# The second part of split weights, finished by an adding DMA instead of VectorE

## The chip, the cores and the metric

The kernel runs on one core of a Trainium2 chip. The metric is the device time of one execution, in microseconds (us); less is better. Engines are named as in the profile: PE is TensorE (PEld its weight loads), DVE is VectorE, ACT is ScalarE, POOL is GpSimd, SP is the engine that issues nearly all DMAs.

## The reference

A two-layer trunk on 512 tokens of width 1024, in float32. Cut to what matters here:

```python
for i in range(DEPTH):                       # 2 layers
    h = rms_norm(x, attn_norm[i])
    proj = h @ w_in[i]                       # one input projection per layer
    mix = diff_attention(...) if i == 0 else gla_attention(...)
    cross = memory_cross_attention(mem_q, mem, mem_norm[i], w_mem_kv[i], mem_qk_norm[i])
    x = x + concat([mix, cross]) @ w_out[i]
    h = rms_norm(x, ffn_norm[i])
    u = causal_conv3(h @ w_up[i]) + conv_b[i]        # depthwise, width 3
    a, g = split(u, 2)
    x = x + (silu(g) * a) @ w_down[i]
```

All large products multiply activations with float32 weights that are read once from DRAM: `w_in`, `w_mem_kv`, `w_out`, `w_up` (1024 x 5632) and `w_down` (2816 x 1024).

## The kernel before, in words

**Products in three parts.** TensorE multiplies in the type float32r, which keeps fewer bits than float32. So each operand is split into a first part (rounded to float32r, `hi`) and a second part (the rest, `lo`), and each product is the sum of three matmuls: hi by hi, hi by lo, lo by hi. In `product` (L262) the weight's `lo` comes third, in `gemm` (L239) second. The matmuls stand at L267 to L269 and at L250 to L252.

**Weight blocks.** The host packs the weights into `wpack`, one block of 128 partitions by up to 1024 columns (`WTILE`) per load, in the order of use. A piece (`_pieces`) is what one step of the program multiplies with, and has one to four blocks: four of 1024 columns for a projection of the attention part (two K tiles of 128 rows each), two for an up-projection (`ua`, `ug`: four K tiles of 256 columns each), three for a down-projection.

**Refilling.** `weights(key)` hands out a piece and makes sure that the next one is already written into the program (`make_piece`). For each block `make_piece` loads a `raw` tile by SP's queue (L207), ACT casts it to `whi` (L200), and DVE subtracts, `wlo` = `raw` - `whi` (L201). There are 3 buffers for `raw`, and 5 (`WB`) each for `whi` and `wlo`. So a block waits for the matmuls that read the block five before it. The first piece and the one after it are made in the opening part, with tiles of their own (L366 to L409).

**Order of the work.** TensorE's instructions keep the order of the program. The other engines' queues are ordered by a scheduler, except in the opening part. In the attention parts a `Filler` queues the units of the projections and puts them between the steps of attention (`F.fill`). In the feed-forward part (`ffn`, L1001) each step q has a piece `ua` and a piece `ug`, used by turns for two output tiles n; ACT and DVE evaluate the convolution from the results (L1017 to L1021), the gate (L1047, L1048) and the split for the next product (L1050, L1051). After six and five steps follow four down-projection pieces each.

**Other users of the queues.** GpSimd has few instructions: memsets of `bt` (L606), `u` (L1005) and others, and sums of squares (L335) in parts of the second layer. SP issues loads and the stores of results.

Of the kernel before, what the change touches and what calls it, by code (L numbers as in the profile page):

```python
# [10 lines left out]
F32 = mybir.dt.float32  # L11
# [3 lines left out]
ALU = mybir.AluOpType  # L15
# [113 lines left out]
def trunk(ctx, tc, x_t, mem_t, wpack, cols_a_d, cols_d, conv_d, gate_d, rel_bias, diff_lambda, consts, onehot, out):  # L129
    nc = tc.nc  # L130
    mm = nc.tensor.matmul
    V, A, G = nc.vector, nc.scalar, nc.gpsimd
# [23 lines left out]
    def blk(b, w=128):  # L156
        return slice(w * b, w * b + w)
# [39 lines left out]
    at = [0]  # L197

    def split_weights(c, raw, hi, lo):
        A.copy(hi[:, c], raw[:, c])  # L200
        V.tensor_sub(lo[:, c], raw[:, c], hi[:, c].bitcast(F32))  # L201

    def raw_tile():
        return wp.tile([128, WTILE], F32, name="raw", tag="raw", bufs=3)

    def load_raw(raw, n):
        nc.sync.dma_start(raw[:, :n], wpack[at[0], :, :n])  # L207
        at[0] += 1
        return raw

    def make_piece(raws=None):
        parts = []
        for i, (_, _, kk, _, w) in enumerate(blocks[len(made)]):
            n = len(kk)
            raw = load_raw(raw_tile(), n * w) if raws is None else raws[i]
            hi, lo = (wp.tile([128, WTILE], F32R, name=t, tag=t, bufs=WB) for t in ("whi", "wlo"))
            split_weights(slice(0, n * w), raw, hi, lo)
            parts += [(hi[:, blk(j, w)], lo[:, blk(j, w)]) for j in range(n)]
        made.append(parts)

# [2 lines left out]
    def weights(key):  # L223
        i = used[0]
        assert plan[i][0] == key, (plan[i][0], key)
        while len(made) < min(i + 2, len(plan)):
            make_piece()
        used[0] += 1
        parts, made[i] = made[i], None
        return parts  # L230
# [123 lines left out]
    with tc.tile_pool(name="ini", bufs=1) as ip, tc.manual_schedule(engines={E.Activation, E.DVE, E.Pool, E.SP}):  # L354
# [11 lines left out]
        raws = [ip.tile([128, WTILE], F32, name=f"raw{i}") for i in range(4)]  # L366
# [34 lines left out]
        for k in range(KT):  # L401
            if k + 1 < KT:
                operands(k + 1)
            if k == 0:
                second.append(load_raw(raws[0], WTILE))
            if k == 4:
                bias_rows(rb, oh, bs)
            if k == KT - 2:
                make_piece(second)  # L409
                weights(("qk", 0))  # L410
                token_rsqrt("lg", acc[0], NB, r_x[:, 0])
                small_vectors()
                for c in range(2):
                    load(bias_d[:, 512 * c:min(512 * c + 512, 640)], bs[c])
            hi, lo = parts[k]
            terms = (xh[k], hi), (xh[k], lo), (xl[k], hi)
            todo = [(b, i) for b in range(NB) for i in range(3)]
            for b, i in sorted(todo, key=lambda bi: bi[1]) if k == 0 else todo:
                xp, w = terms[i]
                mm(first[b], xp[:, blk(b)], w, start=k == 0 and i == 0, stop=k == KT - 1 and i == 2)  # L420
# [736 lines left out]
```

## Time and profile before

| | |
|---|---|
| time, median of 3 runs | 1204.51 us (1204.1 to 1205.91) |
| the profiled execution: time | 1205.31 us |
| the profiled execution: span | 1203.5 us |
| granted TensorE clock | 1.00 |
| read from HBM, written | 112.63 MB, 4.21 MB |

The span runs from the first to the last instruction of the program; the execution's time is somewhat longer. In the profile a group's line has the place in the code, the engine, the operation, what it writes and reads, the count, and then the busy time in us with the mean length of one in ns, and the idle time of the engine just ahead of these instructions with what ended it. The timeline has the start in us, the length in us, then the same names. A matmul's end is modelled: matmuls are shown as 0.39 us long and start every 0.23 us, so their starts are what counts. The line of a DMA issue has the median time from issue to landing at its end; a `DMA ... landing` line has minimum, median and maximum.

### The profile page before, as it was taken

Reading aid. Unit: us, or ns where it says so; the run is one execution under the profiler, and the core shown is the slowest. Engines: PE = TensorE matmul, PEld = TensorE weight load, DVE = VectorE, ACT = ScalarE, POOL = GpSimd, SP = SyncE. Lnnn points to the kernel's source line nnn. Section 1 sums busy time; section 2 is a strip of 40 time slices with the busy share of each in tenths; the row PEclk is TensorE's granted clock in tenths of the full one; section 3 lists DMA queues with packets and bytes.
Section 4 is the critical chain, followed back from the end, with each engine's and each line's share of the span. In section 5 each row is a group of like instructions: output and inputs, shape, how many; then the busy total and the mean of one; then the engine's idle time right before and its main releaser. Section 6 shows DMA issues by size and latency. Waiting matters only on the chain.

```text
span 1203.5 us, 14757 instructions
## 1 busy us (share of the span) xinstructions
PE 1188.3 (99%) x5672; PEld 975.0 (81%) x5672; DVE 759.8 (63%) x1259; ACT 540.7 (45%) x915; POOL 23.5 (2%) x37
## 2 busy tenths in 40 slices
PE   9999999999999999999999999999999999999998
PEld 6887777778888888888787888987888888888887
DVE  7566578887776534767546446768677653476741
ACT  6666666554444222434436444536444432243420
POOL 0000000000000000000020000003000000000000
PEclk9999999999999999999999999999999999999999
DMA  8432231232332331422342221234233233232231
GB/s 275 132 101 84 80 118 49 71 105 88 98 112 70 123 105 53 130 80 88 116 146 74 70 71 57 62 127 133 78 98 112 71 123 97 67 122 84 87 114 44
DMA packets 39413, 117.80 MB, mean 98 GB/s; under 512 B 4688, under 2 KB 5769, under 8 KB 39343
## 3 DMA queue, kind: packets, MB, share of 16 engines
q1 hardware_dynamic: 39198, 116.60, 30.5%
q8 instruction: 44, 0.72, 0.2%
q10 hardware_dynamic: 144, 0.26, 0.1%
q14 instruction: 27, 0.21, 0.1%
HBM read 112.63 MB, written 4.21 MB: 97 GB/s over the span
## 4 chain that ended last, share of the span: by engine, by line
PE 90%; DVE 5%; ACT 3%; issue 1%; DMA 1%; SPq 0%; DVEq 0%; ACTq 0%
PE ps_mm L268 8%; PE ps_mm L269 8%; PE ps_mm L267 8%; PE ps_sm L267 6%; PE ps_sm L268 6%; PE ps_sm L269 6%; PE ps_mm L250 6%; PE ps_mm L252 6%; PE ps_mm L251 5%; PE ps_tp L267 3%; PE ps_tp L268 3%; PE ps_tp L269 3%; PE ps_lg L268 3%; PE ps_lg L269 3%; PE ps_lg L267 3%; PE ps_tp L169 2%
## 5 line engine op out<-in xcount | busy, mean ns | idle before, releaser
L200 ACT CAST whi<-raw 128x1024 fp32r<-128x1024 f32 (+2 forms) x214 | 207.7, 976 | 247.5 <-PE ps_tp L268 133.8
L201 DVE TENSOR_TENSOR wlo<-raw,whi 128x1024 fp32r<-128x1024 f32 (+2 forms) x214 | 240.8, 1136 | 111.0 <-ACT whi L200 109.9
L267 PE MATMUL ps_mm<-xsh,whi 128*128 128x512 f32 x460 | 182.5, 397 | 0.2 <-DVE xt L969 0.2
L268 PE MATMUL ps_mm<-xsl,whi 128*128 128x512 f32 x460 | 179.4, 390 | 1.4 <-DVE xsl L234 1.3
L269 PE MATMUL ps_mm<-xsh,wlo 128*128 128x512 f32 x460 | 179.3, 390 | 0.0
L268 PE MATMUL ps_sm<-xsl,whi 128*128 128x512 f32 x372 | 144.7, 389 | 0.0
L267 PE MATMUL ps_sm<-xsh,whi 128*128 128x512 f32 x372 | 144.7, 389 | 0.0
L269 PE MATMUL ps_sm<-xsh,wlo 128*128 128x512 f32 x372 | 144.7, 389 | 0.0
L250 PE MATMUL ps_mm<-whi,xsh 128*128 128x512 f32 (+2 forms) x352 | 138.2, 393 | 0.1
L252 PE MATMUL ps_mm<-whi,xsl 128*128 128x512 f32 (+2 forms) x352 | 131.4, 373 | 0.3 <-DVE xsl L234 0.3
L251 PE MATMUL ps_mm<-wlo,xsh 128*128 128x512 f32 (+2 forms) x352 | 130.6, 371 | 0.0
L1019 ACT ACTIVATE cvo<-u,cv 128x512 f32<-128x512 f32 x88 | 71.6, 815 | 114.0 <-DVE u L1017 113.6
L268 PEld LDWEIGHTS ps_mm<-xsl,whi 128*128 128x128 f32 x460 | 86.5, 188 | 20.2 <-DVE xsl L234 2.7
L267 PEld LDWEIGHTS ps_mm<-xsh,whi 128*128 128x128 f32 x460 | 86.4, 188 | 18.2 <-DVE xt L969 0.9
L269 PEld LDWEIGHTS ps_mm<-xsh,wlo 128*128 128x128 f32 x460 | 86.3, 188 | 18.1
L1020 DVE SCALAR_TENSOR_TENSOR cvo<-u,cv,cvo 128x512 f32<-128x512 f32 x88 | 65.9, 749 | 31.6 <-ACT cvo L1019 31.4
L268 PEld LDWEIGHTS ps_sm<-xsl,whi 128*128 128x128 f32 x372 | 69.8, 188 | 14.6
L269 PEld LDWEIGHTS ps_sm<-xsh,wlo 128*128 128x128 f32 x372 | 69.8, 188 | 14.5
L267 PEld LDWEIGHTS ps_sm<-xsh,whi 128*128 128x128 f32 x372 | 69.8, 188 | 14.4
L252 PEld LDWEIGHTS ps_mm<-whi,xsl 128*128 128x128 f32 x352 | 66.1, 188 | 12.7 <-DVE xsl L234 0.5
L250 PEld LDWEIGHTS ps_mm<-whi,xsh 128*128 128x128 f32 x352 | 66.3, 188 | 10.7 <-issue 0.9
L251 PEld LDWEIGHTS ps_mm<-wlo,xsh 128*128 128x128 f32 x352 | 66.5, 189 | 9.5
(247 smaller groups left out, 1767.9 us busy)
## 6 DMA issues: line engine op xcount, KB each, us to landing
raw<-in_wpack_dram SPq DMA_DIRECT2D x176, 512.0 KB, 3.5
raw<-in_wpack_dram SPq DMA_DIRECT2D x27, 256.0 KB, 3.5
xt<-in_x_t_dram SPq DMA_DIRECT2D x16, 256.0 KB, 5.3
xres<-xt SPq DMA_DIRECT2D x8, 256.0 KB, 3.5
xt<-xres SPq DMA_DIRECT2D x8, 256.0 KB, 4.4
out_dram<-xt SPq DMA_DIRECT2D x8, 256.0 KB, 2.0
bt<-bias_d SPq DMA_DIRECT2D x6, 256.0 KB, 5.2
raw<-in_wpack_dram SPq DMA_DIRECT2D x4, 384.0 KB, 2.9
```

Source lines behind the costliest of these rows:

```text
L169: nc.tensor.transpose(dst, src, ident[:n, :n])
L200: A.copy(hi[:, c], raw[:, c])
L201: V.tensor_sub(lo[:, c], raw[:, c], hi[:, c].bitcast(F32))
L250: mm(p, sh[k][:, blk(b)], hi, start=k == 0, stop=False)
L251: mm(p, sh[k][:, blk(b)], lo, start=False, stop=False)
L252: mm(p, sl[k][:, blk(b)], hi, start=False, stop=k == KT - 1)
L267: mm(p, hi[:, blk(n)], bh, start=i == first, stop=False)
L268: mm(p, hi[:, blk(n)], bl, start=False, stop=False)
L269: mm(p, lo[:, blk(n)], bh, start=False, stop=i == last)
L1019: A.activation(c, u[:, 2:], AF.Identity, scale=cv[l][:, 2, j:j + 1], bias=cv[l][:, 3, j:j + 1])
L1020: V.scalar_tensor_tensor(c, u[:, 1:S + 1], cv[l][:, 1, j:j + 1], c, op0=ALU.mult, op1=ALU.add)
```

## The change

In `make_piece`, for all blocks but those of the opening, `wlo` is made in another way. ACT casts `raw` to `whi` as before. Then ACT writes the negative of `whi` into `wlo`, and a DMA on GpSimd's queue reads the same block from `wpack` in DRAM once more and adds it onto `wlo`. `wlo` = -`whi` + block is the value that the subtraction gave. A `raw` tile has then only the cast as its reader. DVE has no part in these blocks any more. The blocks of the opening still go through `split_weights`.

```diff
     def make_piece(raws=None):
         parts = []
         for i, (_, _, kk, _, w) in enumerate(blocks[len(made)]):
             n = len(kk)
+            c = slice(0, n * w)
             raw = load_raw(raw_tile(), n * w) if raws is None else raws[i]
             hi, lo = (wp.tile([128, WTILE], F32R, name=t, tag=t, bufs=WB) for t in ("whi", "wlo"))
-            split_weights(slice(0, n * w), raw, hi, lo)
+            if raws is None:
+                A.copy(hi[:, c], raw[:, c])
+                A.mul(lo[:, c], hi[:, c].bitcast(F32), -1.0)
+                G.dma_start(lo[:, c], wpack[at[0] - 1, :, c], accum_op=ALU.add)
+            else:
+                split_weights(c, raw, hi, lo)
             parts += [(hi[:, blk(j, w)], lo[:, blk(j, w)]) for j in range(n)]
         made.append(parts)
```

## The prediction

> **What bounds the kernel now.** I read the page first, then who waited for whom, then the timeline of single weight blocks.
>
> ```profile
> span 1203.5 us, 14757 instructions
> PE 1188.3 (99%) x5672; PEld 975.0 (81%) x5672; DVE 759.8 (63%) x1259; ACT 540.7 (45%) x915; POOL 23.5 (2%) x37
> ...
> q1 hardware_dynamic: 39198, 116.60, 30.5%
> ...
> PE 90%; DVE 5%; ACT 3%; issue 1%; DMA 1%; SPq 0%; DVEq 0%; ACTq 0%
> ...
> L200 ACT CAST whi<-raw 128x1024 fp32r<-128x1024 f32 (+2 forms) x214 | 207.7, 976 | 247.5 <-PE ps_tp L268 133.8
> L201 DVE TENSOR_TENSOR wlo<-raw,whi 128x1024 fp32r<-128x1024 f32 (+2 forms) x214 | 240.8, 1136 | 111.0 <-ACT whi L200 109.9
> ...
> raw<-in_wpack_dram SPq DMA_DIRECT2D x176, 512.0 KB, 3.5
> ```
>
> TensorE is busy 99% of the span and holds 90% of the chain that ended last. VectorE is busy for 63%. So the 241 us that L201 takes on VectorE are not on the path that sets the end, and taking them away can return only what TensorE now waits. That is little: in the answer for L201 the only one who waited for a wlo is a weight load, for 0.4 us, and the largest waits of the weight loads for VectorE are two short lines.
>
> ```profile
> who waited for it (us, times):
>   PEld ps_lg L613: 0.4, 1
> ...
> PEld ps_mm L268 <- DVE xsl L234: 2.7, 3, 1.6
> PEld ps_lg L800 <- DVE xt L805: 2.1, 2, 1.3
> ```
>
> What matters is how long a refilled block takes. There are five whi and five wlo buffers, so a block can only be refilled when TensorE has let go of the one five blocks earlier, and then has a limited margin until TensorE wants it.
>
> **What changes for a block.** The instruction order of the built kernel shows 203 blocks changed, 172 of them 128x1024; TensorE's order is the same. For each, VectorE's subtraction goes. ScalarE gets a second instruction of the same size, GpSimd's queue an issue, and the DMA engines a second reading of the block from DRAM, added into SBUF. The prices nearest to these:
>
> ```profile
> L207 SPq DMA_DIRECT2D raw<-in_wpack_dram x207: 327/328/587, 13.1 to 1169.2; - x104
> DMA to landing us min/median/max: 2.0/3.5/5.7
> L335 POOL TENSOR_TENSOR xt<-xt 128x512 f32<-128x512 f32 x12 | 19.1, 1588 | 380.0 <-ACT xt L333 375.7 <-issue 3.7 <-POOL xt L335 0.4
> L333 ACT ACTIVATE xt<-xt 128x512 f32<-128x512 f32 x36 | 22.0, 621 | 0.0
> ```
>
> *The negative.* It is a 128x1024 pass on ScalarE like the cast, which the timelines below show at 1.05 us; an activation of half that width takes 0.62 us, so at most some 1.3. I take 1.05, high end 1.5. In all that is about 200 us more for ScalarE (L200 takes 207.7): 740 us, 61%. Its length is hidden under matmuls; its latency is not.
>
> *The issue.* The trace has no DMA on GpSimd's queue. Bounds: 0.33 us, as on SP, and 1.6 us, as a tensor operation there. I take the middle, 1.0. Between the additions stand only memsets of bt and, in the second layer, L335 sums, each among blocks with time to spare.
>
> *The adding transfer.* The trace has none of these either. Payload first: the queue of the loads held 30.5% of 1203.5 us for 116.6 MB, so a 512 KB load (0.524 MB) holds the engines 1.65 us. An addition has two operands, the block in DRAM and what stands in SBUF; as two such streams it is 3.3 us, which I take. Ends: 1.65 (the second stream free) and 4.95 (two reads and the write one after the other). Landing: the load's median 3.5 us plus another 1.65 is 5.2; ends 3.5 and 7.0. The Trainium skill, "Collectives: The Full Stack" (section "The bandwidth ceiling"), says that a reducing transfer runs at half a copy's rate, because of its two source reads and not of the sum; by it 3.3 is right. The skill's "DMA: Bandwidth & Descriptors" (section "Anatomy of one DMA — SWDGE (gpsimd) path") gives about 2.0 us plus the bytes over 436 GB/s for a DMA of GpSimd; taken over both streams that is an estimated 4.4 us in place of my 5.2, and the forecast below would be about 20 us lower. No run so far shows which.
>
> So from the end of the cast to a finished wlo: now 1.23 us, after the change 1.05 + 1.0 + 5.2 = 7.25, that is 6.0 later. And each block holds the DMA engines 1.65 + 3.3 = 4.95 us, where it held them 1.65; blocks refilled close together wait for each other at that pace.
>
> **Stage by stage.** Each fence shows casts, subtractions and the matmuls that first read the part in question.
>
> First layer's attention, one piece of four blocks (the last three refilled together):
>
> ```profile
> 51.54 1.05 ACT L200 CAST whi<-raw 128x1024 fp32r<-128x1024 f32 x1 [0.52 <-PE ps_mm L252]
> 55.13 1.05 ACT L200 CAST whi<-raw 128x1024 fp32r<-128x1024 f32 x1 [0.30 <-PE ps_mm L252]
> 56.22 1.23 DVE L201 TENSOR_TENSOR wlo<-raw,whi 128x1024 fp32r<-128x1024 f32 x1 [0.55 <-ACT whi L200]
> 58.03 0.39 PE L251 MATMUL ps_mm<-wlo,xsh 128*128 128x512 f32 x1
> 62.06 0.39 PE L251 MATMUL ps_mm<-wlo,xsh 128*128 128x512 f32 x1
> ```
>
> The cast waits for TensorE, so it can't start earlier. Third block: wlo done at 57.45, first read at 62.06, a margin of 4.6 us. New: the first block is issued at 51.54 + 2.1 + 1.0 = 54.64 and lands at 59.84, already 1.8 after 58.03; the third lands 9.9 later at 69.7, 7.7 after 62.06. Five pieces in this layer have such margins (4.2 to 5.8 by the same reading): 5 x 7.7 = 39 us.
>
> Second layer's projections, third block of the tightest of six pieces:
>
> ```profile
> 706.21 1.03 ACT L200 CAST whi<-raw 128x1024 fp32r<-128x1024 f32 x1
> 706.45 2.35 DVE L201 TENSOR_TENSOR wlo<-raw,whi 128x1024 fp32r<-128x1024 f32 x2
> 712.42 0.39 PE L251 MATMUL ps_mm<-wlo,xsh 128*128 128x512 f32 x1
> ```
>
> The margin is 3.6 (708.8 to 712.4). I take 7 us for three pieces like it and 1 for the other three, whose blocks lie further apart: 24 us.
>
> First layer's up-projections, one pair of pieces:
>
> ```profile
> 478.13 2.00 ACT L200 CAST whi<-raw 128x1024 fp32r<-128x1024 f32 x2
> 480.02 0.81 ACT L1019 ACTIVATE cvo<-u,cv 128x512 f32<-128x512 f32 x1
> 483.08 2.12 ACT L200 CAST whi<-raw 128x1024 fp32r<-128x1024 f32 x2 [2.24 <-issue]
> 479.46 2.35 DVE L201 TENSOR_TENSOR wlo<-raw,whi 128x1024 fp32r<-128x1024 f32 x2
> 483.51 0.39 PE L269 MATMUL ps_sm<-xsh,wlo 128*128 128x512 f32 x1
> 484.19 0.39 PE L269 MATMUL ps_mm<-xsh,wlo 128*128 128x512 f32 x1
> 489.63 0.39 PE L269 MATMUL ps_mm<-xsh,wlo 128*128 128x512 f32 x1
> ```
>
> In the new order both casts come before the first negative: it ends at 478.13 + 2.0 + 1.05 = 481.2, lands at 487.4, and 484.19 becomes 487.4: 3.2 us. For the second pair of casts a convolution's activation (0.81) and the second cast also stand ahead of the negative: landing 493.25 against 489.63 + 3.2, another 0.4. Of eleven pairs I count ten: 36 us.
>
> Second layer's up-projections, where three blocks are refilled 2.7 us apart with a larger margin, and down-projections (last two lines):
>
> ```profile
> 895.25 1.06 ACT L200 CAST whi<-raw 128x1024 fp32r<-128x1024 f32 x1 [0.89 <-PE ps_sm L268]
> 896.21 0.63 ACT L1047 ACTIVATE cvo<-cvo 128x512 f32<-128x512 f32 x1
> 902.29 1.22 DVE L201 TENSOR_TENSOR wlo<-raw,whi 128x1024 fp32r<-128x1024 f32 x1
> 912.05 0.39 PE L269 MATMUL ps_mm<-xsh,wlo 128*128 128x512 f32 x1
> ...
> 980.86 1.23 DVE L201 TENSOR_TENSOR wlo<-raw,whi 128x1024 fp32r<-128x1024 f32 x1 [2.96 <-ACT whi L200]
> 991.32 0.39 PE L269 MATMUL ps_lg<-midh,wlo 128*128 128x512 f32 x1
> ```
>
> First block: 895.25 + 1.05 + 0.63 + 1.05 + 1.0 + 5.2 = 904.2; the third 9.9 later, 914.1, 2.0 after 912.05. Nine pairs: 18 us. Down: 982.1 + 6.0 = 988.1, before 991.32: nothing. The same holds for the output projections, whose blocks are small and early.
>
> Sum: 39 + 24 + 36 + 18 = 117 us of new TensorE waits, less some 3 us of those for VectorE: +114. The profiled execution took 1205.3 us (1.8 outside its span), 0.8 above the median of 1204.5: **1319 us** for the forecast.
>
> Low end (0.33, 3.5, and 3.3 us per block): third block at 51.54 + 2.1 + 0.33 + 3.5 + 6.6 = 64.1, 2.0 late, five times 10; second layer's three pieces 8; up-projections 485.0 against 484.19, 8; else nothing: 26 less 3, **1228**. High end (1.5, 1.6, 7.0, and 6.6 us per block): 5 x 13.8 = 69, 48, ten times 6.5 = 65, nine times 8.2 = 74, and in the down-projections three blocks hold the engines 19.8 us where TensorE needs 72 matmuls at 0.227 (483.51 to 484.19 are three), 16.4: fourteen times 3.4, 48. Together 304: **1509**.
>
> **Rivals.**
> 1. *The DMA engines become the bound.* For: nothing shows that an addition keeps to twice a load, and from 3.8 us on (5.45 for 24 matmuls less 1.65) the feed-forward stages run at the engines' pace. Against: the engines are now at 30.5%. Time: the high end, about 1510, more if the addition is slower still. Chance 0.28.
> 2. *Faster.* The addition lands as quickly as the fastest load, 2.0 us: 1.05 + 0.33 + 2.0 = 3.4 from cast to wlo, 2.2 later than now, inside every margin above (3.5 from 480.7 to 484.19 is the tightest). Then only relief is left: VectorE's queue is a third shorter, and the two rows of waits for it, 4.8 us, and the smaller ones like them shrink. Place: the start of the second layer and the first output projection; price about -5, 1199. It decides while cast to wlo stays under some 4.7 us. Against: a median load alone takes 3.5. Chance 0.05.
> 3. *Nothing to see.* Margins hold and relief is under 2 us: 1204. Chance 0.03. Just above it, a few pieces late, 1208 to 1235: 0.06.
>
> That the change doesn't do what it says is excluded by the order: 203 subtractions are gone from VectorE.
>
> The forecast itself, 1235 to 1420, has 0.58. **Range** 1225 to 1520: it leaves out rivals 2 and 3, part of the cases just above, and a third of rival 1. A change of 0.2% (2.4 us) is about what a measurement of this kernel can tell from none. Faster 0.05, same 0.03, slower 0.92.
>
> **What the profile after would show.** VectorE about 540 us, ScalarE about 740, twice the bytes read from DRAM, TensorE's share falling to about 90% with waits of L251 and L269 for a DMA of wlo: some 8 us once per projection piece in the attention stages, 3 to 4 per pair in the first feed-forward, 2 in the second. I am wrong if TensorE stays at 99%, if its waits end on casts instead of additions, or if the waits come at every block alike, which would be rival 1.

## The result, and the profile after

The changed kernel takes 1350.38 us (median of four runs, 1343.61 to 1361.32), the kernel before 1204.3 us beside it: 1.122 times as long, with an interval of 1.114 to 1.130. It is slower by 146 us where 115 were forecast. The profiled execution is the fastest of the four, 1343.61 us, and the sums below by engine and by stage are made with it; run against run, medians are compared. In `make_piece` the cast is now L220, the negative L221, the adding transfer L222. Lines behind it are 7 higher than before: the matmuls of `gemm` are L257 to L259, those of `product` L274 to L276.

From the page of the changed kernel, the lines that answer to those of before:

```profile
span 1341.8 us, 15146 instructions
PE 1234.7 (92%) x5672; PEld 995.0 (74%) x5672; DVE 551.5 (41%) x1056; ACT 719.2 (54%) x1118; POOL 196.4 (15%) x240
PEclk9998999999898999998999999999999999999999
q0 software_dynamic: 29232, 98.64, 40.5%
q1 hardware_dynamic: 39198, 116.60, 25.3%
...
L222 POOL DMA_DIRECT2D wlo<-in_wpack_dram x203 | 175.6, 868 | 1034.3 <-ACT wlo L221 901.9
L221 ACT ACTIVATE wlo<-whi 128x1024 fp32r<-128x1024 f32 (+4 forms) x203 | 199.6, 991 | 2.5
...
raw<-in_wpack_dram SPq DMA_DIRECT2D x176, 512.0 KB, 5.1
wlo<-in_wpack_dram POOLq DMA_DIRECT2D x172, 512.0 KB, 8.3
```

Start with TensorE's line. It runs the same 5672 matmuls, and yet it is busy for 1234.7 us, not for 1188.3. So the 138.3 us that the span grew have two parts: TensorE idles 91.9 us more (107.1 against 15.2), and its matmuls take 46.4 us longer. The clock line points to most of the second part: four of the forty slices are at 8, and the mean granted clock of the span is 0.972, where it was 1.00. The last line has the other finding: an addition lands 8.3 us after its issue, and a load, which took 3.5 us in the kernel before, now needs 5.1.

Who waited, from the changed kernel's answer on TensorE's waits (us in total, times, the longest):

```profile
PE ps_mm L276 <- DMA wlo<-in_wpack_dram: 49.4, 27, 4.6
PE ps_mm L258 <- DMA wlo<-in_wpack_dram: 40.9, 20, 4.6
```

These 90.3 us are nearly all of the idle time that was added, and they end on the addition, not on a cast.

Stage by stage, from the table of stretches (bounds and length in us, busy time and count of PE, PEld, DVE, ACT and POOL, granted clock, share of the DMA engines, GB/s). The kernel before, first layer's attention and the first group of its up-projections:

```profile
0.00:269.00 269.00, 262.01 (x1383) 207.84 (x1384) 194.13 (x465) 167.52 (x386) 2.15 (x16) 1.00 0.35 113
269.00:395.00 126.00, 126.00 (x555) 103.75 (x554) 92.56 (x119) 56.33 (x71) 0.00 (x0) 1.00 0.30 93
```

The changed kernel: first layer's attention, its first and second group of up-projections, its last down-projections, then the second layer's attention and its first group of up-projections:

```profile
0.00:308.00 308.00, 275.29 (x1385) 213.99 (x1385) 161.95 (x427) 198.06 (x425) 35.95 (x55) 0.97 0.60 154
308.00:470.00 162.00, 138.75 (x554) 110.27 (x555) 67.10 (x95) 76.36 (x93) 18.69 (x22) 0.93 0.58 143
...
538.00:674.50 136.50, 118.35 (x484) 94.58 (x483) 54.43 (x76) 61.95 (x76) 17.19 (x20) 0.94 0.60 147
674.50:730.00 55.50, 55.50 (x241) 44.90 (x240) 13.66 (x19) 32.40 (x44) 18.39 (x18) 1.00 0.96 228
730.00:970.00 240.00, 219.76 (x1169) 185.69 (x1167) 106.55 (x231) 135.40 (x236) 40.99 (x50) 0.97 0.60 144
970.00:1104.00 134.00, 127.90 (x557) 103.56 (x556) 67.57 (x96) 80.03 (x96) 19.70 (x23) 1.00 0.71 173
```

The second of these rows stands for the whole: the same 555 matmuls that filled 126 us now take 162, because TensorE idles 23 us and works at a clock of 0.93. The fourth row is the opposite case: in these down-projections the DMA engines are busy for 96% and TensorE doesn't wait at all. By such stretches the stages grew: first attention by 39 us, first up-projections by 63, second attention by 24, second up-projections by 11.5, down-projections by less than 1.

One wait closely, in the first layer's up-projections: ScalarE's timeline, GpSimd's, the transfer in the chain of the changed kernel (start, length, what), the row of that stretch in the table of stretches, then TensorE's timeline:

```profile
325.67 2.00 ACT L220 CAST whi<-raw 128x1024 fp32r<-128x1024 f32 x2 [0.17 <-PE ps_sm L275]
327.57 0.81 ACT L1026 ACTIVATE cvo<-u,cv 128x512 f32<-128x512 f32 x1
328.29 2.00 ACT L221 ACTIVATE wlo<-whi 128x1024 fp32r<-128x1024 f32 x2
```

```profile
329.63 1.81 POOL L222 DMA_DIRECT2D wlo<-in_wpack_dram  x2 [2.97 <-ACT wlo L221]
```

```profile
329.63 9.11 DMA wlo<-in_wpack_dram
```

```profile
329.63:338.74 9.11, 4.83 (x22) 3.64 (x20) 3.89 (x6) 2.61 (x4) 1.72 (x2) 0.95 1.06 268
```

```profile
338.78 0.79 PE L276 MATMUL ps_mm<-xsh,wlo 128*128 128x512 f32 x1 [4.32 <-DMA wlo<-in_wpack_dram]
339.38 0.63 PE L274 MATMUL ps_mm<-xsh,whi 128*128 128x512 f32 x1
339.80 0.63 PE L275 MATMUL ps_mm<-xsl,whi 128*128 128x512 f32 x1
...
345.02 0.39 PE L276 MATMUL ps_mm<-xsh,wlo 128*128 128x512 f32 x1
345.25 0.39 PE L274 MATMUL ps_mm<-xsh,whi 128*128 128x512 f32 x1
```

TensorE lets go of the first `whi` buffer, and the casts start at 325.67. Two casts, an activation of the convolution and the first negative later, at 329.63, the addition is issued, and it lands at 338.74. TensorE has waited 4.32 us for it. Over these 9.11 us the DMA engines have no free time (a share of 1.06 as the profile counts it) and move 268 GB/s, which is 2.4 MB, more than four blocks of 0.524 MB. It is so in every wait: in the table of stretches the share is between 0.96 and 1.18 in each of TensorE's 49 waits for a `wlo`, the 47 above and two short ones (for waits under 1 us, in the microsecond that ended them), while over the whole span it is 66%. Then see the starts: 339.38, 339.80, each 0.43 us after the one before, and so on to 344.5; at 345 they follow each other at 0.23 again. After the wait the matmuls run at about half speed for over 5 us.

### The profile page after: what moved, and what is told of

It is laid out like the page before. It is cut to its first block, busy times and chain, and to the rows that moved or that the text cites. A ratio compares the mean times of both kernels' runs of the same rounds, so it can differ in the third digit from the quotient of the medians.

```text
span 1341.8 us, 15146 instructions
## 1 busy us (share of the span) xinstructions
PE 1234.7 (92%) x5672; PEld 995.0 (74%) x5672; DVE 551.5 (41%) x1056; ACT 719.2 (54%) x1118; POOL 196.4 (15%) x240
## 3 DMA queue, kind: packets, MB, share of 16 engines
q0 software_dynamic: 29232, 98.64, 40.5%
q1 hardware_dynamic: 39198, 116.60, 25.3%
## 4 chain that ended last, share of the span: by engine, by line
PE 46%; issue 30%; DMA 14%; POOL 5%; ACT 3%; DVE 1%; POOLq 0%; SPq 0%; ACTq 0%; DVEq 0%
DMA wlo<-in_wpack_dram 14%; POOL wlo L222 5%; PE ps_mm L276 4%; PE ps_mm L274 3%; PE ps_mm L275 3%; PE ps_mm L258 3%; PE ps_sm L276 3%; PE ps_mm L259 3%; PE ps_sm L274 3%; PE ps_sm L275 3%; PE ps_mm L257 3%; PE ps_tp L169 2%; PE ps_lg L275 1%; PE ps_lg L274 1%; PE ps_lg L276 1%
## 5 line engine op out<-in xcount | busy, mean ns | idle before, releaser
L222 POOL DMA_DIRECT2D wlo<-in_wpack_dram x203 | 175.6, 868 | 1034.3 <-ACT wlo L221 901.9
L220 ACT CAST whi<-raw 128x1024 fp32r<-128x1024 f32 (+4 forms) x203 | 197.5, 984 | 155.6 <-PE ps_tp L275 105.5
L276 PE MATMUL ps_mm<-xsh,wlo 128*128 128x512 f32 x460 | 190.2, 414 | 49.6 <-DMA wlo<-in_wpack_dram 49.4
L221 ACT ACTIVATE wlo<-whi 128x1024 fp32r<-128x1024 f32 (+4 forms) x203 | 199.6, 991 | 2.5
L274 PE MATMUL ps_mm<-xsh,whi 128*128 128x512 f32 x460 | 188.8, 410 | 0.0
L275 PE MATMUL ps_mm<-xsl,whi 128*128 128x512 f32 x460 | 185.7, 404 | 0.0
L258 PE MATMUL ps_mm<-wlo,xsh 128*128 128x512 f32 (+2 forms) x352 | 138.0, 392 | 41.0 <-DMA wlo<-in_wpack_dram 40.9
L276 PEld LDWEIGHTS ps_mm<-xsh,wlo 128*128 128x128 f32 x460 | 90.5, 197 | 80.9 <-DMA wlo<-in_wpack_dram 62.1
L274 PE MATMUL ps_sm<-xsh,whi 128*128 128x512 f32 x372 | 144.7, 389 | 0.0
L276 PE MATMUL ps_sm<-xsh,wlo 128*128 128x512 f32 x372 | 144.7, 389 | 0.0
L257 PE MATMUL ps_mm<-whi,xsh 128*128 128x512 f32 (+2 forms) x352 | 142.5, 405 | 0.0
L259 PE MATMUL ps_mm<-whi,xsl 128*128 128x512 f32 (+2 forms) x352 | 135.6, 385 | 0.0
L258 PEld LDWEIGHTS ps_mm<-wlo,xsh 128*128 128x128 f32 x352 | 69.2, 197 | 59.8 <-DMA wlo<-in_wpack_dram 50.5
L275 PEld LDWEIGHTS ps_mm<-xsl,whi 128*128 128x128 f32 x460 | 90.2, 196 | 19.9 <-issue 0.5
L274 PEld LDWEIGHTS ps_mm<-xsh,whi 128*128 128x128 f32 x460 | 90.9, 198 | 18.3 <-issue 0.5
L276 PEld LDWEIGHTS ps_sm<-xsh,wlo 128*128 128x128 f32 x372 | 69.8, 188 | 14.5
L274 PEld LDWEIGHTS ps_sm<-xsh,whi 128*128 128x128 f32 x372 | 69.8, 188 | 14.5
L1024 DVE TENSOR_TENSOR u<-ps_mm,rB 128x512 f32<-128x512 f32 x44 | 30.3, 691 | 121.3 <-PE ps_mm L276 121.1
```

The costliest lines, as they stand in the source:

```text
L221: A.mul(lo[:, c], hi[:, c].bitcast(F32), -1.0)
L222: G.dma_start(lo[:, c], wpack[at[0] - 1, :, c], accum_op=ALU.add)
L257: mm(p, sh[k][:, blk(b)], hi, start=k == 0, stop=False)
L258: mm(p, sh[k][:, blk(b)], lo, start=False, stop=False)
L259: mm(p, sl[k][:, blk(b)], hi, start=False, stop=k == KT - 1)
L274: mm(p, hi[:, blk(n)], bh, start=i == first, stop=False)
```

## The experiments

Every edit is made to the changed kernel unless something else is said. "Before" ran beside each group, at 1205.87 and 1205.44 us in the two timed groups. The stage figures come from the same cuts as above.

### ScalarE's pass without the transfer

```diff
-                G.dma_start(lo[:, c], wpack[at[0] - 1, :, c], accum_op=ALU.add)
+                V.tensor_add(lo[:, c], raw[:, c], lo[:, c].bitcast(F32))
```

> The negative on ACT stays, but DVE adds the raw block instead of the DMA; nothing is read twice. Theory A (the time goes to waiting for the adding transfer): ACT's 203 extra passes (199.6 us busy) lie beside matmuls; wlo is about 1.05 us later than in the kernel before, inside every margin (tightest 3.5 us), so 1204 to 1208 us. Rival B (ACT's second pass and the order of its queue cost the time): a large part of the 146 us is still there, 1250 us or more.

Measured: 1225.65 us (1223.54 to 1227.53), 1.017 [1.015, 1.019]. Neither expectation held. With no transfer at all, the second pass on ScalarE and VectorE's sum behind it cost 20 us. Both feed-forward parts take as long as before, but the first attention takes 13.5 us more and the second 7.3. There TensorE waits for short steps, as in this kernel's answer on waits; two rows of VectorE's timeline stand behind the first of them:

```profile
PE ps_lg L807 <- DVE xsh L797: 2.5, 1, 2.5
PE ps_lg L620 <- ACT r_mem L190: 1.9, 1, 1.9
```

```profile
662.77 1.22 DVE L222 TENSOR_TENSOR wlo<-raw,wlo 128x1024 fp32r<-128x1024 f32 x1 [1.50 <-ACT wlo L221]
664.03 0.68 DVE L797 TENSOR_TENSOR xsh<-ps_tp,xsh 16x512 fp32r<-16x512 f32 x1
```

VectorE's step L797 starts when the sum ahead of it has ended, and that sum had waited 1.50 us for a negative. ScalarE's step L190 starts at 95.39, right behind a negative that began at 94.43. So ScalarE's pass delays its own queue, and in this run VectorE's too. The changed kernel has no such sum on VectorE. How the 20 us are made up beyond these waits isn't shown.

Its TensorE is busy for 1196.6 us (8.3 more than before) at a clock of 0.993, and idle for 14 more: again both parts.

### A transfer that copies in place of one that adds

```diff
-                G.dma_start(lo[:, c], wpack[at[0] - 1, :, c], accum_op=ALU.add)
+                G.dma_start(lo[:, c], wpack[at[0] - 1, :, c])
```

> As the changed kernel, but GpSimd's DMA copies the block over wlo instead of adding it; the second part is then the whole weight, and the addition is left out. Same issue, same bytes from DRAM, same waits. If the second stream (what is read back from SBUF for the sum) costs what the trace suggests (a 512 KB addition holds the engines 2.9 us, a load 1.5 us): landing falls from 8.3 us to about 5, the waits for it from 91 us to about 25, the time to about 1235 us. If GpSimd's way of issuing is the cost and not the addition, landing stays near 8 us and the time near 1350 us.

Measured: 1264.96 us (1261.03 to 1267.45), 1.049 [1.046, 1.052], where about 1235 was expected. The landing fell as far as expected, TensorE's waits for it only to 40 us and not to 25. From its page:

```profile
q0 software_dynamic: 29232, 98.64, 25.0%
...
wlo<-in_wpack_dram POOLq DMA_DIRECT2D x172, 512.0 KB, 5.0
```

With the run before this gives a ladder of kernels: ScalarE's pass with VectorE's sum 20 us, GpSimd's transfer in place of that sum 39 us more, adding in place of copying 85 us more. These are differences between kernels, not costs of parts that could be added in another order. The same bytes hold the engines for 25.0% of 1263.7 us, 316 us, when they are copied and for 40.5% of 1341.8 us, 543 us, when they are added: 1.7 times as long. The copy lands in 5.0 us, the addition in 8.3.

### The transfers by themselves

To the kernel before, behind its last stage, 18 transfers of 512 KB are added, each waiting for the one before it: a load of SP, a copy of GpSimd, an addition of GpSimd, six times.

> The kernel before, and behind its end 18 transfers of 512 KB from DRAM into one tile, each after the landing of the last: by turns a load on SP's queue, a copy on GpSimd's queue and an addition on GpSimd's queue, with nothing beside them. If the 8.3 us of the additions come from sharing the engines with the loads: about 3.4, 4 and 5 us from issue to landing. If the addition itself is slow: about 3.4, 4 and 8 us. The time of this kernel is longer by the 18 transfers, some 90 us, and means nothing else.

Answers for the line of the copies and for the line of the additions:

```profile
L1090 POOL DMA_DIRECT2D tend<-in_wpack_dram x6: 550/554/724, 1202.2 to 1268.0; - x6
...
DMA to landing us min/median/max: 3.7/3.8/3.9
```

```profile
L1092 POOL DMA_DIRECT2D tend<-in_wpack_dram x6: 861/868/873, 1206.3 to 1272.1; - x6
...
DMA to landing us min/median/max: 5.3/5.4/5.4
```

Alone, an addition lands 5.4 us after its issue, 1.6 after a copy would. So the 8.3 us in the changed kernel aren't its own length: 2.9 of them come from what runs beside it. A load of SP lands in 3.5 us here too. The share of the DMA engines over an addition's 5.4 us is 0.56 to 0.61 here, where it was 1.06 in the wait shown above. The issue of an addition holds GpSimd for 0.87 us, that of a copy for 0.55.

### Without the loads beside it

Cut to the place that loads; `keep_raw` is a list that starts empty.

```diff
-            raw = load_raw(raw_tile(), n * w) if raws is None else raws[i]
+            if raws is None:
+                if len(keep_raw) < 3:
+                    keep_raw.append(load_raw(raw_tile(), WTILE))
+                else:
+                    at[0] += 1
+                raw = keep_raw[at[0] % len(keep_raw)]
+            else:
+                raw = raws[i]
```

> As the changed kernel, but the raw tiles are loaded three times only and then cast again and again: the 200 further loads on SP's queue are left out, and the weights are wrong. What remains is the same chain with the DMA engines to itself. If the additions are late because loads share the engines: landing falls from 8.3 us to under 6, the waits for wlo from 91 us to about 35, the time to about 1265 us. If the addition is slow by itself: landing 7 us or more, 1320 us or more.

Measured: 1272.39 us (1268.84 to 1275.27), 1.055 [1.053, 1.058]. From its page and from its answer on waits (lines are 7 higher again):

```profile
wlo<-in_wpack_dram POOLq DMA_DIRECT2D x172, 512.0 KB, 5.6
```

```profile
PE ps_mm L283 <- DMA wlo<-in_wpack_dram: 23.4, 11, 2.7
PE ps_mm L265 <- DMA wlo<-in_wpack_dram: 21.1, 18, 2.9
```

With 200 loads gone the additions land in 5.6 us, TensorE's waits for them halve (44.5 us in place of 90.3), and 78 us of the 146 are gone. So over half of the loss goes when the loads do: additions and loads share the DMA engines. The engines are busy for only 66% of the span (40.5 and 25.3), but for all of the time in the waits: it is the few microseconds after each release that are crowded, not the span. The kernel whose transfers only copy lands them in 5.0 us and loses 59 us; this one lands in 5.6 and loses 67; the changed kernel lands in 8.3 and loses 146. The 78 us of this run and the 85 of adding in place of copying are not two separate parts: each takes work from the engines in the same waits.

### The change in the second layer's feed-forward part alone

```diff
-            if raws is None:
+            if raws is None and plan[len(made)][0][0] in ("ua", "ug", "dn") and plan[len(made)][0][1] == 1:
```

> The change for the weight blocks of the second layer's feed-forward part alone; all others are split as before. If the loss is made where margins are short, then this costs what the trace shows for these stages, +7 to +12 us (up-projections 8.2 us of waits, down-projections none): 1211 to 1217 us, with the granted clock at 1.00. If the additions hurt everywhere by their traffic (half of all additions are here), it costs some 40 us or more: 1245.

Measured: 1214.45 us (1211.85 to 1216.74), 1.007 [1.006, 1.009], inside the expectation. From its page:

```profile
PEclk9999999999999999999999999999999999999999
...
L276 PE MATMUL ps_mm<-xsh,wlo 128*128 128x512 f32 x460 | 180.8, 393 | 6.5 <-DMA wlo<-in_wpack_dram 6.5
...
wlo<-in_wpack_dram POOLq DMA_DIRECT2D x64, 512.0 KB, 8.1
```

A third of the additions (the expectation had said half), landing as late as in the changed kernel, cost 9 us, where a third of the loss would be 49. In the profiled run the up-projections are 10 us longer and the down-projections no longer. The loss is made where margins are short, not by the traffic. And waits of at most 1.1 us leave the clock at 1.00.

### The second part read last

```diff
         for i in ids:
             (hi, lo), (bh, bl) = parts[i], pairs[i]
             mm(p, hi[:, blk(n)], bh, start=i == first, stop=False)
             mm(p, hi[:, blk(n)], bl, start=False, stop=False)
+        for i in ids:
+            (hi, lo), (bh, bl) = parts[i], pairs[i]
             mm(p, lo[:, blk(n)], bh, start=False, stop=i == last)
```

> As the changed kernel, but in the products of the feed-forward and output projections all matmuls with the weight's first part come before those with its second part. The first reading of a wlo in an up-projection then comes 14 matmuls (3.2 us at 0.227) later; the projections of the attention parts keep their order. Theory A: the feed-forward waits for DMAs (39 us in the first layer, 5.5 us in the second, by the trace) fall to under 10 us, and the half-clock windows that follow them (41 us long, half of it lost) mostly go too: about 1290 us, granted clock 0.985. Rival C (the DMA engines' throughput is the bound): the waits only move, and the time stays within 10 us of 1350.

Measured: 1332.06 us (1330.72 to 1335.18), 1.106 [1.104, 1.108], 18 us less than the change and not the 60 expected; between the two profiled executions it is 11 us, and the stages below go by these. The first layer's up-projections, two groups of pieces:

```profile
308.00:455.00 147.00, 133.52 (x556) 106.70 (x555) 67.52 (x95) 78.18 (x95) 19.00 (x22) 0.97 0.67 159
524.00:652.50 128.50, 116.53 (x482) 92.93 (x481) 54.16 (x76) 63.14 (x77) 18.09 (x21) 0.96 0.66 155
```

They take 275.5 us in place of 298.5, so a later first reading does help there, and the second layer's gain 5.5; the engines' work for the whole stage was no bound, or nothing could have been gained. But TensorE still idles 25 us, and the second attention loses 8 us, the down-projections about 9. In the second attention the idle time is as in the changed kernel (19.9 us against 20.2); its matmuls are slower, at a clock of 0.92 in place of 0.97, and why is open. For the down-projections a likely cause, argued and not shown: a `wlo` that is read last is also let go last, so its refill begins later.

### Work for TensorE in the waits

```diff
+            if l == 0 and i % 4 == 0 and i:
+                for _ in range(12):
+                    mm(p, xh[0][:, 0:128], xh[0], start=True, stop=True)
```

> As the changed kernel, but in the first layer's up-projections, ahead of the first product of each pair after the first, TensorE runs 12 more matmuls (2.7 us at full clock) whose result is overwritten. They stand where it would wait for wlo. Theory D (a wait of about 3 us or more is followed by 3.4 us or more at half clock, which is a loss of its own): the waits shrink by the 2.7 us that the extra matmuls take, the half-clock windows between 330 and 660 us (41 us) mostly vanish, and the kernel is 5 to 20 us faster in spite of 120 more matmuls. If the lower clock comes from load and not from the waits, it gets no faster and up to 30 us slower.

Measured: 1348.23 us (1342.35 to 1351.28), 1.118 [1.115, 1.121]: no difference to the change, where 5 to 20 us less was expected. The same two groups:

```profile
310.00:469.50 159.50, 145.28 (x616) 116.45 (x615) 67.33 (x95) 76.52 (x93) 18.84 (x22) 0.98 0.59 144
538.50:678.00 139.50, 128.06 (x543) 103.00 (x541) 54.41 (x76) 62.02 (x76) 16.97 (x20) 0.98 0.59 144
```

They hold 120 more matmuls, 27 us of TensorE at 0.2275 us each, and take 299.0 us against 298.5. Busy time rose by only 16.2 us (273.3 against 257.1), so the kernel's own matmuls took 11 us less: the clock is 0.98 in place of 0.93 and 0.94. More work, higher clock: the clock falls for the waits, not for the load. Idle time fell by 15.7 us, not by 27. Why not more, and whether the clock's 11 us would count in full without the filling, stays open.

### The negative on VectorE

```diff
-                A.mul(lo[:, c], hi[:, c].bitcast(F32), -1.0)
+                V.tensor_scalar_mul(lo[:, c], hi[:, c].bitcast(F32), -1.0)
```

> As the changed kernel, but DVE writes the negative instead of ACT; the adding DMA stays. With ACT's pass and DVE's sum alone the kernel took 1226 us, 20 more than before, nearly all in the two attention stages (+13.5, +7.3). If that is ACT's pass standing ahead of other work in its queue, then moving it to DVE (13% less busy) gives back some 10 to 20 us of the 1350: 1330 to 1340. If it was the new order of the queues, little comes back: 1345 to 1355. Rival F, a page rule (the Trainium skill, SBUF — State Buffer, on DVE blocking GpSimd's DMAs): a one-source float32 pass of DVE inside SBUF keeps GpSimd from writing its transfers, so GpSimd's issue (868 ns) and the landing (8.3 us) get longer and the time rises above 1360.

Measured: 1343.48 us (1342.64 to 1350.69), 1.116 [1.113, 1.120], an interval that overlaps the change's. From its page:

```profile
L222 POOL DMA_DIRECT2D wlo<-in_wpack_dram x203 | 180.9, 914 | 1016.9 <-DVE wlo L221 795.5
...
L221 DVE TENSOR_SCALAR wlo<-whi 128x1024 fp32r<-128x1024 f32 (+4 forms) x203 | 133.4, 662 | 123.2 <-ACT whi L220 118.7
...
wlo<-in_wpack_dram POOLq DMA_DIRECT2D x172, 512.0 KB, 9.1
```

A negative of 0.66 us in place of 0.99, and ScalarE back at 540 us, bring nothing that can be told from zero, and the time lies between the two forecasts. So no 20 us for ScalarE's pass can be taken out of the changed kernel in this way. A likely reason, not shown: where TensorE waits for an addition anyway, the small delays of ScalarE don't show; and part of the 20 us came from VectorE's sums, which the changed kernel lacks. The issue got 46 ns longer and the landing 0.8 us, as rival F says, but the time didn't rise: a later landing doesn't always cost time.

### Waits of chosen length

To the kernel before, behind its last stage, 18 bursts of 60 matmuls are added, with a chain of copies on ScalarE between two bursts (cut to the loop; `gl` and `gr` are 128x512 tiles of zeros, `tmp` a tile for the copies):

```diff
+        for g in (1, 8, 2, 7, 3, 6, 4, 5, 1, 8, 2, 7, 3, 6, 4, 5, 4, 4):
+            p = bank("mm")
+            for i in range(60):
+                mm(p, gl[:, blk(0)], gr, start=i == 0, stop=i == 59)
+            A.copy(tmp, p)
+            for i in range(g - 1):
+                A.copy(tmp[:, :448], tmp[:, :448])
+            A.copy(gr[:, :64], tmp[:, :64])
```

> The kernel before, whole, and behind its last stage 18 bursts of 60 equal matmuls (128x128 by 128x512, zeros) on TensorE; between two bursts TensorE waits for a chain of ACT copies, 2 to 9 of them, so for some 1 to 5 us, in the order 1 8 2 7 3 6 4 5 1 8 2 7 3 6 4 5 4 4 of the chain's length; no DMA and no other engine works then. The theory that waits of TensorE alone bring the half clock: after waits under about 2 us the burst keeps its 0.2275 us from one matmul to the next and lasts 13.7 us; after waits over about 2.4 us it starts at 0.427 us a matmul, for 3.4 or 6.8 us, and lasts 15.3 to 17 us; the change between the two lies at one length and not at random. The rival, that the clock falls because the DMA engines, GpSimd and ScalarE work beside TensorE in the changed kernel: no slow matmuls here after any of the waits, all bursts 13.7 us.

TensorE's timeline, each row one burst with the wait ahead of it in brackets:

```profile
1237.28 16.47 PE L1095 MATMUL ps_mm<-gr,gl 128*128 128x512 f32 x60 [5.18 <-ACT gr L1099]
1255.35 13.90 PE L1095 MATMUL ps_mm<-gr,gl 128*128 128x512 f32 x60 [1.60 <-ACT gr L1099]
...
1291.61 13.94 PE L1095 MATMUL ps_mm<-gr,gl 128*128 128x512 f32 x60 [2.48 <-ACT gr L1099]
...
1436.88 15.49 PE L1095 MATMUL ps_mm<-gr,gl 128*128 128x512 f32 x60 [2.20 <-ACT gr L1099]
...
1475.31 15.27 PE L1095 MATMUL ps_mm<-gr,gl 128*128 128x512 f32 x60 [2.79 <-ACT gr L1099]
```

No DMA and no other engine runs beside these bursts, and they slow down all the same, so waits alone are enough and the rival falls. Of the 18, the four behind waits up to 1.60 us last 13.9 us; all eleven behind waits of 2.79 us and more last 15.3 to 16.5, so they lose 1.4 to 2.6 us each. In between it isn't one length that decides, though that was expected: 2.20 us brought a slow burst, 2.48 and 2.59 did not. The Trainium skill, "TensorE: Matmul & The Clock Gate" (section "What's actually happening"), says that the clock falls to half after an idle window of about 3.4 us, and that the windows run freely, whatever the kernel does. That the outcome between 2.2 and 2.6 us is mixed agrees with free windows; that 2.2 us can be enough differs from the 3.4, and here the measurement decides.

## Why the prediction was right, and where it wasn't

The direction and the mechanism were right. VectorE is at 551.5 us (540 said), ScalarE at 719.2 (740), TensorE at 92% (90), the weight is read twice, the waits are those of L251 and L269 (now L258 and L276) for `wlo`, and they come in the stages named and hardly in the others (two waits, 0.9 us together).

**The payload** was right: 543 us of the engines for 98.64 MB are 2.9 us for a block of 0.524 MB, against 3.3 taken. A load holds them 25.3% of 1341.8 us for 116.6 MB, 1.53 us; the ratio is 1.9, and to a copy by GpSimd's queue it was 1.7. So the rule of half a copy's rate in the Trainium skill, "Collectives: The Full Stack" (section "The bandwidth ceiling"), holds here roughly for an addition into SBUF. **The issue** was put at 1.0 and took 0.87.

**The landing** was too short. From issue to landing the sum had 1.0 + 5.2 = 6.2 us; alone it is 5.4, in the kernel 8.3. The prediction let each further block of a group come 4.95 us later, a load and an addition, but it let the first addition of a group land as if nothing ran beside it, and in the up-projections of the first layer it is that one that counts. Without the loads the landing is 5.6, and 78 us are gone: this is the largest thing the sum had too small. In the wait shown above, cast to landing took 13.1 us (325.67 to 338.74), where the prediction's steps for a pair (2.0 + 0.8 + 1.05 + 1.0 + 5.2) give 10.1.

**The stage sums.** First up-projections: 36 us of waits said, 41.4 found (idle time of the two rows above). Second ones: 18 said, 8.2 of waits and 11.5 of time found. The attention stages: 39 and 24 said, and the times did grow by 39 and 24, but not for the reason given: the idle time there was 26 and 16 longer, less than said, and slower matmuls made up the rest: TensorE's busy time in the first attention rose from 262.0 to 275.3. That the times agree is luck. The sum had let three blocks follow each other at 4.95 us each, so that the last would be 7.7 us late. In the changed kernel three waits in a row of the first attention end at 98.70, 102.58 and 106.35, so 3.8 to 3.9 us apart, and the longest wait of TensorE is 4.6. So two errors of the sum worked against each other: a landing that was too short and a pace that was too slow. In all 117 us of waits were said and 92 found.

**The missing term** is that of matmuls that run slower after a wait. Neither the sum nor a rival had it. TensorE's busy time grew by 46.4 us. At most 37.6 of them are the clock, (1 - 0.972) x 1341.8; most of the rest is the end of the pipeline, which shows at every wait: 47 waits with a last matmul shown 0.39 us long, not covered after 0.2275, are 7.6 us. How much of the clock's loss reaches the end isn't settled by the sum alone: the four runs of the changed kernel have clocks of 0.972, 0.962, 0.952 and 0.961 and times of 1343.6, 1352.0, 1361.3 and 1348.8, so from the first to the third run the clock's loss grew by 28 us and the time by 18. This is likely also why the changed kernel scatters by 1.3% and the one before by 0.2%; no run tested it.

So 1319 was 25 us under the profiled run and 31 under the median: 117 us of waits became 92, and 46 us of slower matmuls weren't in it.

**Hidden work.** "Its length is hidden under matmuls; its latency is not" was half the truth for ScalarE's pass: without a transfer, and with VectorE's sum behind it, it costs 20 us in the attention stages, in steps other than the weights. In the change itself such a cost can't be seen, as the run with the negative on VectorE shows.

**Rival 1**, the DMA engines as the bound of whole stages, is refuted by the down-projections, where they are busy for 96% and TensorE never waits, and by the run with the second part read last, which is faster at the same bytes. But it had a true part: in the waits themselves the engines are full (0.96 to 1.18), and without the loads the waits halve. **Rivals 2 and 3** fall with a landing of 5.4 us alone: cast to `wlo` is 1.05 + 5.4 = 6.5 us or more, where rival 2 needed under 4.7. The Trainium skill, "DMA: Bandwidth & Descriptors" (section "Anatomy of one DMA — SWDGE (gpsimd) path"), gave an estimated 4.4 us in place of the 5.2, the issue not counted. The additions by themselves agree: 5.4 less 0.87 for the issue are 4.5. It is the loads beside them that the estimate doesn't have, and the kernel's 7.4 (8.3 less 0.87) lies above both.

Nothing that was run beats the kernel before, and there is little to beat: it keeps TensorE at 99%.

## What to carry to other kernels

Before moving work off an engine that isn't the bound, ask what the bound waits for when a buffer is refilled, and measure the new path from release to ready against that margin: in the wait shown the first block of a pair took 13.1 us from the first cast, where in a pair of the kernel before it needed 2.6 (478.13 to 480.7 in the prediction's rows). Price a transfer by its landing beside the transfers that run with it, not alone, and look at the share of the DMA engines in the wait and not over the span. And by the bursts measured here a wait of TensorE of 2.8 us or more costs more than its length: add 1.4 to 2.6 us for the half-speed matmuls behind it, so many short waits are cheaper than a few long ones.

## What the runs showed of the hardware that was not expected

- TensorE's clock falls to half after waits that are shorter than 3 us: in 18 bursts always from 2.79 us on, once in three between 2.20 and 2.59, never up to 1.60, and in the changed kernel the matmuls then start every 0.43 us, in the wait shown for 5.7 us.
- An addition of 512 KB from DRAM into SBUF lands in 5.4 us alone, a copy by the same queue in 3.8, a load by SP in 3.5; in the changed kernel, beside loads, the addition needs 8.3 and at most 11.4 us.
- Issuing an addition holds GpSimd for 0.87 us, a copy of the same size for 0.55.
- The DMA engines can be busy for 66% of the span and yet be full (a share of 0.96 to 1.18) in each of the 49 waits for an addition.
